# Twelve key pages instead of five handed out in layer 0's w_out, and the second sixteen hand-outs moved from page 200 to page 212

## The chip, the cores and the metric

The kernel runs on one core of one Trainium2 chip. The metric is the device time of one execution in microseconds: before the change 2924.34 us, the median of three runs (2919.79 to 2924.56). A core has a matrix engine (PE; PEld is its loading of weights), a vector engine (DVE), a scalar engine (ACT), GpSimd (POOL) and a sequencer that mostly issues DMA (SP). Each takes its instructions in the order in which they stand in its own list, and waits on semaphores for what the others have to finish first.

## The reference

One inference step of two layers over a prompt of 1024 tokens plus 16 meta tokens, and over 8 running sequences that add one token each. Layer 0 mixes with gated linear attention, layer 1 with differential attention; each is followed by a squared-ReLU MLP and post-norms. The part that the change touches is the attention of the 8 running sequences over their cached keys and values, 32 pages of 128 rows each, found through a page table. All is float32.

```python
def diff_core(q, k, v, q_pos, k_pos, lam):
    s = jnp.einsum('bqhmd,bkhmd->bhmqk', q, k).astype(F32) * (DIFF_DH ** -0.5)
    mask = k_pos[None, :] <= q_pos[:, None]
    s = jnp.where(mask, s, -jnp.inf)
    p = jax.nn.softmax(s, axis=-1)
    a = p[:, :, 0] - lam * p[:, :, 1]
    return jnp.einsum('bhqk,bkhe->bqhe', a, v.astype(F32))

def diff_sample(x, cache_k, cache_v, page_table, w_in, lam, lam_init, g_sub, w_out):
    ...
    k_past = cache_k[page_table].reshape(B, past, DIFF_HEADS, 2, DIFF_DH).astype(k.dtype)
    v_past = cache_v[page_table].reshape(B, past, DIFF_HEADS, DIFF_DV).astype(v.dtype)
    k_all = jnp.concatenate([k_past, k], axis=1)
    v_all = jnp.concatenate([v_past, v], axis=1)
    o = diff_core(q, k_all, v_all, pos, jnp.arange(past + T), lam)
```

## The kernel before

The prompt's work is matrix products of 128x128 tiles. Each float32 operand is split into a rounded high part and a rest (XH and XL, whi and wlo, HH and HL), and a product is three matmuls on these (`mm3`, L185 to L188). The stages in question follow each other: the output projection of layer 0 (`w_out`, 16 tiles), its post-norm and transposes (`normalize`, `to_fm`), layer 0's MLP (`mlp`, 8 groups, in each 8 tiles up and 16 down), the input projections of layer 1 (12 units of weights x 4 tiles, L1047 on), then differential attention over the prompt (`prep`, `tile_`). A tile is 48 matmuls of 256 columns, or 24 of 512, into one of three PSUM buffers (mmt). ACT and DVE take it out: L902 in w_out, the split into HH and HL (L183) for the MLP's first product, L1014 for its second, L1060 and the rope's L1068 to L1071 in the projections (for the units of queries and keys, the first 32 tiles).

Beside this runs the decode of the 8 sequences (`decode`). A key page is loaded (512 KB, `page`, L758, one of 8 buffers named pg), multiplied by the sequence's query row qb (L789; three of four pages on DVE, the fourth on POOL) and reduced to scores (L790, DVE). qb is one buffer: the row of the next sequence (L778) is loaded once the last multiply of the one before has read it. After 32 pages comes a softmax (`soft`: L795 a maximum on DVE, L797 and L801 on PE with L799 on DVE between, L802 on DVE, an exponential on ACT, L804 on DVE, L806 on PE, then L808 to L813 on DVE). The value pages of a sequence go with the key pages of the next: they are loaded into the same 8 buffers and multiplied by the weights on PE (L830). At the end of a sequence ACT, PE (L844) and DVE (L846) store its output. Keys are counted through: page 32 b + n is page n of sequence b, so 256 in all. SP reads each page's number from a table in memory (L756) before it issues its load; the tables and page buffers are given up when the projections end, and attention's tiles, among them its mask (cmask, L1102), take their place.

What sets the order: the program is written as one stream, and when it is built a scheduler lays it out on the engines by a simulated timeline. Decode's page work has the lowest priority, so it is put where an engine would otherwise have nothing. Where that comes too early, the source ties an instruction behind another one (`tc.issue_after`). `decode` is a generator, and handing out a page means that the prompt's code calls `next` on it once: in `w_out` after each of the first tiles, in the MLP's first group after every second tile of its second product (8 times), and in the projections after every tile. It stops (`yield`) before each page of sequence 0, and before 16 pages from HOLD on. A multiply of a page of sequence 0 up to page 23, and of a page of HOLD's sequence from HOLD's page on, is tied behind the latest step recorded in `steps_v` (L902, L1014, L1071 and others) at the time of its hand-out. After the MLP's first group the generator is run on to the first stop of HOLD, with no hand-outs between; after the 16th of the second set it runs to its end.

Of the kernel before, what the change touches and what calls it, by code (L numbers as in the profile page):

```python
# [30 lines left out]
NPG = 32  # L31
# [2 lines left out]
NEG = -1e30  # L34
LAM_INIT = 0.8 - 0.6 * math.exp(-0.3)
PGB = 8
HOLD = (6, 8)
HTB = 1
LEVELS = (64, 32, 16, 8, 4, 2, 1)
ROPE_INV = 500000.0 ** (-np.arange(0, 16, 2, dtype=np.float64) / 16)  # L40
# [70 lines left out]
def hybrid_step(ctx, tc, A, dbg=None, upto=9):  # L111
# [14 lines left out]
    def mmt():  # L126
        return mm.tile([P, 512], F32, name="mmt")
# [4 lines left out]
    def smt():  # L132
        return sm.tile([P, 512], F32, name="smt")
# [44 lines left out]
    def kunit(w, c0):  # L178
        return unit(256, w.rearrange("(k p) n -> p k n", p=P)[:, :, c0 : c0 + 256])
# [431 lines left out]
    for h in range(GH):  # L611
# [7 lines left out]
        for c in range(2):  # L619
# [3 lines left out]
            b = g2.tile([P, 512], F32, name="gb")  # L623
# [105 lines left out]
    @contextmanager  # L729
    def background():  # L730
        at = tc.cur_priority
        tc.cur_priority = bg_at[0]
        yield
        bg_at[0] = tc.cur_priority
        tc.cur_priority = at
# [17 lines left out]
    def page(cache, b, n):  # L753

        with tc.issue_after(gathers[-4]) if len(gathers) > 3 else nullcontext():
            r = nc.sync.value_load(ptab[b : b + 1, n : n + 1], min_val=0, max_val=A["cache_k"].shape[1] - 1)  # L756
        t = pgp.tile([P, D], F32, name="pg")
        gathers.append(dma(t, A[cache][0, ds(r, 1)].rearrange("a p h d -> (a p) (h d)")).ins)  # L758
        return t
# [14 lines left out]
    def k_start(b):  # L774
        sc = dp2.tile([P, NPG + 1, 16], F32, name="sc")
        qb = dp.tile([P, D], F32, name="qb")
        with background():
            dma(qb, A["qs"][b : b + 1, :].broadcast_to([P, D]))  # L778
            V.memset(sc[:, NPG, :], NEG)
            V.tensor_scalar(sc[:NS, NPG, :], own, other[:NS, b : b + 1], None, ALU.add)  # L780
        return sc, qb

    def k_page(b, n, sc, qb):
        with background():
            pg = page("cache_k", b, n)
            eng, after = (G, steps_g) if n % 4 == 3 else (V, steps_v)

            with tc.issue_after(after[-1]) if (b == 0 and n < 24 and after) or (b == HOLD[0] and HOLD[1] <= n) else nullcontext():
                eng.tensor_tensor(pg, pg, qb, op=ALU.mult)  # L789
            return V.tensor_reduce(sc[:, n, :], pg.rearrange("p (h d) -> p h d", d=64), op=ALU.add, axis=AX.X).ins  # L790

    def soft(sc):

        mx = dp.tile([P, 16], F32, name="mx")
        V.tensor_reduce(mx, sc.rearrange("p n c -> p c n"), op=ALU.max, axis=AX.X)  # L795
        ps = smt()
        TE.transpose(ps[:16, :P], mx, ident)  # L797
        m1 = dp.tile([16, 1], F32, name="m1")
        V.tensor_reduce(m1, ps[:16, :P], op=ALU.max, axis=AX.X)  # L799
        ps = smt()  # L800
        TE.matmul(ps[:, :16], m1.broadcast_to([16, P]), ident[:16, :16], start=True, stop=True)  # L801
        V.tensor_tensor(sc, sc, bc(ps[:, :16], [P, NPG + 1, 16], 1), op=ALU.subtract)  # L802
        S.activation(sc, sc, AF.Exp, scale=0.125)
        V.tensor_reduce(mx, sc.rearrange("p n c -> p c n"), op=ALU.add, axis=AX.X)  # L804
        ps = smt()
        TE.matmul(ps[:, :16], one, mx, start=True, stop=True)  # L806
        cf = dp.tile([P, 16], F32, name="cf")
        V.reciprocal(cf, ps[:, :16])  # L808
        cv = cf.rearrange("p (c m) -> p c m", m=2)
        V.tensor_tensor(cv, cv, bc(lamv, [P, 8, 2], 1), op=ALU.mult)  # L810
        V.tensor_tensor(sc, sc, bc(cf, [P, NPG + 1, 16], 1), op=ALU.mult)
        av = sc.rearrange("p n (c m) -> p n c m", m=2)
        V.tensor_tensor(av[:, :, :, 0], av[:, :, :, 0], av[:, :, :, 1], op=ALU.add)  # L813
        return sc
# [10 lines left out]
    def v_pages(pages, w, acc, behind):  # L825

        for n, pg in pages:
            r = slice(0, P if n < NPG else 32)
            for i in range(4):
                m = TE.matmul(acc[i * TS : i * TS + 16, :256], w[r, n, :], pg[r, i * 256 : (i + 1) * 256], start=n == 0, stop=n == NPG).ins  # L830
                if behind is not None:

                    tc.add_manual_dep(m, behind.name, mybir.DependencyInfo(mybir.DependencyClass.NoSync, mybir.DependencyReason.DATA), reason="order")
                    behind = None
# [13 lines left out]
    def decode():  # L848
        ks = None
        for b in range(NS + 1):  # L850
            prev = ks
            if b < NS:
                ks = k_start(b)
            if b > 0:
                w = soft(prev[0])
                acc = smt()
            held, k = [], None
            for n in range(NPG):
                if b == 0 or (b == HOLD[0] and HOLD[1] <= n < HOLD[1] + 16):
                    yield b  # L860
                if b < NS:
                    k = k_page(b, n, *ks)
                if b > 0:

                    if len(held) == 2:
                        v_pages(held, w, acc, k)
                        held = []
                    held.append((n, v_load(b - 1, n)))
            if b > 0:
                held.append((NPG, v_load(b - 1, NPG)))  # L870
                v_pages(held, w, acc, None)
                v_end(b - 1, acc)
# [9 lines left out]
    def w_out(w, scaled, side=None):  # L882

        units = {}
        n = 0
        for u, c in ((0, 0), (1, 0), (0, 1), (1, 1), (2, 0), (3, 0), (2, 1), (3, 1)):
            if u not in units:
                units[u] = kunit(w, u * 256)
            hv, lv = (x.rearrange("p (k n) -> p k n", n=256) for x in units[u])
            for i2 in range(2):  # L890
                ps = mmt()
                t0 = 4 * c + 2 * i2
                for i in range(2):
                    a = slice((t0 + i) * P, (t0 + i + 1) * P)
                    for k in range(NB):
                        mm3(ps[:, i * 256 : (i + 1) * 256], XH[:, k, a], XL[:, k, a], hv[:, k, :], lv[:, k, :], k == 0, k == NB - 1)
                yv = Yt[:, t0 : t0 + 2, u * 256 : (u + 1) * 256]
                pv = ps.rearrange("p (i n) -> p i n", n=256)
                if scaled:
                    V.tensor_tensor(yv, yv, pv, op=ALU.add)  # L900
                else:
                    steps_v.append(V.scalar_tensor_tensor(yv, yv, ALPHA, pv, ALU.mult, ALU.add).ins)  # L902
                if side and (n == 4 if scaled else n < 5):
                    next(side)
                n += 1
                if u % 2:
                    for t in (t0, t0 + 1):
                        yield t, u // 2
# [663 lines left out]
```

## Time and profile before

| what | value |
| --- | --- |
| three runs | 2924.56, 2924.34, 2919.79 us |
| span of the profiled execution | 2919.67 us |
| mean granted PE clock | 0.976 |
| read from and written to HBM | 575.55 MB and 44.06 MB |

The span runs from the first to the last instruction of the profiled execution. It lies 0.12 us below the lowest of the three runs; the median lies 4.7 us above it. On the time axis of the profile w_out runs from about 525 to 615 us, the MLP from there to about 1440, the projections of layer 1 from about 1453 to 1785, and attention over the prompt follows. In a row of a timeline stand start, length, engine, source line and operands, and in brackets how long the engine was idle just before and what ended that. A row of waits gives the total, the number and the longest. In a group's row stand the busy time and the mean length of one in ns, then the idle time ahead.

### The profile page before, as it was taken

How to read it: one execution, taken by the hardware profiler on the slowest of the kernel's cores; microseconds unless marked ns; L12 is line 12 of the kernel's file. 1: busy time of each engine (PE TensorE's matmuls, PEld its weight loads, DVE VectorE, ACT ScalarE, POOL GpSimd, SP SyncE). 2: the span in 40 equal slices, each digit the busy share in tenths (PEclk: the TensorE clock that was granted, in tenths of full speed). 3: DMA queues.
4: the chain of work that ended last, by engine and by line, in shares of the span. 5: the costliest groups of instructions: out<-in, count | busy, mean ns of one | idle time of the engine just before them, and what ended most of it. 6: DMA issues, size and time to landing. Idle time of an engine off the chain costs nothing. (4 is left out here: it accounts for less than half of the span.)

```text
span 2919.7 us, 52085 instructions
## 1 busy us (share of the span) xinstructions
PE 2779.7 (95%) x19653; PEld 2277.6 (78%) x19653; DVE 1891.2 (65%) x2982; ACT 1044.1 (36%) x2075; POOL 1133.7 (39%) x867
## 2 busy tenths in 40 slices
PE   8889999999999999999999998889998999999997
PEld 5666767987777777777898896778888889797885
DVE  2564644457877777777667942788638855838478
ACT  3233453251222122122321112667524535335352
POOL 2230222233333334334233331132335766677664
PEclk9899999999999999999999998999999999999998
DMA  7557651514798988988387999363436778595893
GB/s 257 178 185 251 233 177 37 198 56 141 242 350 297 335 309 298 346 317 321 137 275 252 348 343 314 75 139 86 119 112 205 195 207 232 152 281 129 257 246 87
DMA packets 285366, 636.46 MB, mean 218 GB/s; under 512 B 25510, under 2 KB 141292, under 8 KB 273852
## 3 DMA queue, kind: packets, MB, share of 16 engines
q1 hardware_dynamic: 252716, 520.66, 51.6%
q0 software_dynamic: 32400, 112.50, 15.9%
q8 instruction: 154, 2.52, 0.4%
q14 instruction: 96, 0.79, 0.1%
HBM read 575.55 MB, written 44.06 MB: 212 GB/s over the span
## 5 line engine op out<-in xcount | busy, mean ns | idle before, releaser
L174 POOL TENSOR_TENSOR wlo<-raw,whi 128x512 fp32r<-128x512 f32 x256 | 360.0, 1419 | 744.0 <-ACT whi L173 670.8
L186 PE MATMUL mmt<-whi,XH 128*128 128x256 f32 (+1 forms) x1760 | 527.4, 302 | 2.9 <-ACT Y L310 2.0
L187 PE MATMUL mmt<-wlo,XH 128*128 128x256 f32 (+1 forms) x1760 | 527.8, 301 | 0.7 <-POOL wlo L174 0.7
L186 PE MATMUL mmt<-XH,whi 128*128 128x512 f32 (+1 forms) x1216 | 438.1, 361 | 7.4 <-DVE HL L183 7.2
L188 PE MATMUL mmt<-whi,XL 128*128 128x256 f32 x1536 | 437.2, 286 | 0.1
L188 PE MATMUL mmt<-XH,wlo 128*128 128x512 f32 (+1 forms) x1216 | 434.4, 358 | 0.0
L790 DVE TENSOR_REDUCE sc<-pg 128x16 f32<-128x1024 f32 x256 | 309.7, 1214 | 93.4 <-POOL pg L789 90.1
L173 ACT CAST whi<-raw 128x512 fp32r<-128x512 f32 x256 | 152.9, 619 | 578.4 <-PE mmt L188 191.1
L186 PEld LDWEIGHTS mmt<-whi,XH 128*128 128x128 f32 x1760 | 333.4, 190 | 30.1 <-issue 15.6
L187 PEld LDWEIGHTS mmt<-wlo,XH 128*128 128x128 f32 x1760 | 334.8, 190 | 28.2 <-issue 16.8
L187 PE MATMUL mmt<-XL,whi 128*128 128x512 f32 x768 | 307.3, 400 | 0.0
L188 PEld LDWEIGHTS mmt<-whi,XL 128*128 128x128 f32 x1536 | 292.1, 191 | 9.9 <-issue 8.8
L789 DVE TENSOR_TENSOR pg<-pg,qb 128x1024 f32<-128x1024 f32 x192 | 256.8, 1343 | 62.1 <-DMA pg<-in_cache_k 38.1
L186 PEld LDWEIGHTS mmt<-XH,whi 128*128 128x128 f32 x1216 | 231.7, 191 | 55.1 <-issue 13.7
L789 POOL TENSOR_TENSOR pg<-pg,qb 128x1024 f32<-128x1024 f32 x64 | 158.6, 2478 | 293.5 <-DMA pg<-in_cache_k 236.7
L188 PEld LDWEIGHTS mmt<-XH,wlo 128*128 128x128 f32 x1216 | 231.8, 191 | 35.8 <-issue 3.8
L186 PE MATMUL mmt<-whi,HH 128*128 128x512 f32 x512 | 205.6, 402 | 1.7 <-DVE Y L1014 1.7
L187 PE MATMUL mmt<-wlo,HH 128*128 128x512 f32 x512 | 204.7, 400 | 0.0
L188 PE MATMUL mmt<-whi,HL 128*128 128x512 f32 x512 | 203.9, 398 | 0.0
L187 PEld LDWEIGHTS mmt<-XL,whi 128*128 128x128 f32 x768 | 145.4, 189 | 39.6 <-issue 8.8
L1416 POOL TENSOR_TENSOR wlo<-RW,whi 128x512 fp32r<-128x512 f32 x96 | 156.3, 1749 | 37.1 <-ACT whi L1415 37.0
L1416 POOL TENSOR_TENSOR wlo<-rw,whi 128x512 fp32r<-128x512 f32 x92 | 147.7, 1674 | 41.4 <-ACT whi L1415 41.2
(441 smaller groups left out, 5769.3 us busy)
## 6 DMA issues: line engine op xcount, KB each, us to landing
pg<-in_cache_k SPq DMA_DIRECT2D x256, 512.0 KB, 6.0
pg<-in_cache_v SPq DMA_DIRECT2D x256, 512.0 KB, 6.0
XH<-xc POOLq DMA_DIRECT2D x42, 1032.0 KB, 7.9
raw<-in_mlp_w SPq DMA_DIRECT2D x164, 256.0 KB, 3.5
swt<-in_mlp_w SPq DMA_DIRECT2D x32, 1024.0 KB, 5.6
rw<-in_mlp_w SPq DMA_DIRECT2D x116, 256.0 KB, 3.8
RW<-in_mlp_w POOLq DMA_DIRECT2D x96, 256.0 KB, 6.0
xc<-XH POOLq DMA_DIRECT2D x14, 1032.0 KB, 6.8
```

Source lines behind the costliest of these rows:

```text
L173: S.copy(hi[:, c], raw)
L174: G.tensor_tensor(lo[:, c], raw, hi[:, c].bitcast(F32), op=ALU.subtract)
L186: TE.matmul(ps, ah, bh, start=first, stop=False)
L187: TE.matmul(ps, ah, bl, start=False, stop=False)
L188: TE.matmul(ps, al, bh, start=False, stop=last)
L789: eng.tensor_tensor(pg, pg, qb, op=ALU.mult)
L790: return V.tensor_reduce(sc[:, n, :], pg.rearrange("p (h d) -> p h d", d=64), op=ALU.add, axis=AX.X).ins
L1416: G.tensor_tensor(lo[:, k, :], t, hi[:, k, :].bitcast(F32), op=ALU.subtract)
```

## The change

```diff
-HOLD = (6, 8)
+HOLD = range(212, 228)
...
-            with tc.issue_after(after[-1]) if (b == 0 and n < 24 and after) or (b == HOLD[0] and HOLD[1] <= n) else nullcontext():
+            with tc.issue_after(after[-1]) if (b == 0 and n < 24 and after) or HOLD.start <= NPG * b + n < NPG * (HOLD.start // NPG + 1) else nullcontext():
                 eng.tensor_tensor(pg, pg, qb, op=ALU.mult)
...
-                if b == 0 or (b == HOLD[0] and HOLD[1] <= n < HOLD[1] + 16):
+                if b == 0 or NPG * b + n in HOLD:
                     yield b
...
-                if side and (n == 4 if scaled else n < 5):
+                if side and (n == 4 if scaled else n < 12):
                     next(side)
```

In `w_out` of layer 0 `next` is called after 12 tiles, before after 5. The first call only starts the generator, so 11 key pages are handed out there (pages 0 to 10), before 4. The 8 calls in the MLP's first group then hand out pages 11 to 18, before 4 to 11. The second set of 16 is pages 212 to 227, before 200 to 215; it now goes over the change from sequence 6 to sequence 7 at page 224. Tied behind a step are pages 212 to 223, before 200 to 223.

No instruction is added or removed; the order on the engines changes. Counted in DVE's list by reduces (L790): ahead of the last tile of w_out stand 11 of them, before 4; ahead of the end of the MLP's first group 25, before 14; of its second group 46, before 39; of its end 212, before 200; of the projections' tile 12 there are 224, before 212; of tile 16 231, before 216; of tile 32 255, before 240.

The first place is DVE at the end of the MLP's first group. L1014 takes out its last tile and the HL rows are the splits of the second group's first tiles; pg and sc are decode's. Before:

```order
L1014 TENSOR_TENSOR Y<-Y,mmt 128x512 x2
L789 TENSOR_TENSOR pg<-pg,qb 128x1024 x8
L790 TENSOR_REDUCE sc<-pg 128x16 x5
L183 TENSOR_TENSOR HL<-mmt,HH 128x512
L790 TENSOR_REDUCE sc<-pg 128x16 x3
L183 TENSOR_TENSOR HL<-mmt,HH 128x512
```

and now:

```order
L1014 TENSOR_TENSOR Y<-Y,mmt 128x512
L789 TENSOR_TENSOR pg<-pg,qb 128x1024 x3
L790 TENSOR_REDUCE sc<-pg 128x16
L789 TENSOR_TENSOR pg<-pg,qb 128x1024
L790 TENSOR_REDUCE sc<-pg 128x16 x4
L183 TENSOR_TENSOR HL<-mmt,HH 128x512
L790 TENSOR_REDUCE sc<-pg 128x16 x2
L183 TENSOR_TENSOR HL<-mmt,HH 128x512
```

Between the last L1014 and the first HL there were eight multiplies and five reduces, and there are four and five; the multiplies taken out stand among the rows ahead.

The second place is DVE at the change from sequence 6 to 7, in the projections; qo, qr are the rope's tiles, m is the softmax's maximum. Before, at tile 21 to 24:

```order
L799 TENSOR_REDUCE m_17598<-smt 16x1
L789 TENSOR_TENSOR pg<-pg,qb 128x1024 x2
L1068 TENSOR_TENSOR qo<-mmt,c_rope 128x8x16
L1069 TENSOR_TENSOR qr<-mmt,c_rope 128x8x8
L1070 TENSOR_TENSOR qr<-mmt,c_rope 128x8x8
L802 TENSOR_TENSOR sc<-sc,smt 128x528
L790 TENSOR_REDUCE sc<-pg 128x16
L789 TENSOR_TENSOR pg<-pg,qb 128x1024
L790 TENSOR_REDUCE sc<-pg 128x16
L1071 TENSOR_TENSOR qo<-qo,qr 128x8x16
L804 TENSOR_REDUCE mx<-sc 128x16
```

and now, at tile 12 to 13:

```order
L795 TENSOR_REDUCE mx<-sc 128x16
L789 TENSOR_TENSOR pg<-pg,qb 128x1024
L1068 TENSOR_TENSOR qo<-mmt,c_rope 128x8x16
L1069 TENSOR_TENSOR qr<-mmt,c_rope 128x8x8
L1070 TENSOR_TENSOR qr<-mmt,c_rope 128x8x8
L1071 TENSOR_TENSOR qo<-qo,qr 128x8x16
L779 MEMSET sc 128x16
L790 TENSOR_REDUCE sc<-pg 128x16
L780 TENSOR_SCALAR sc<-own,c_other 8x16
L789 TENSOR_TENSOR pg<-pg,qb 128x1024
L790 TENSOR_REDUCE sc<-pg 128x16
L789 TENSOR_TENSOR pg<-pg,qb 128x1024
```

with L846 and L799 right behind. The first multiply by sequence 7's query row stood behind L799, and now stands behind L795 and ahead of L799 and of a rope. On PE 35 matmuls of the projections stand between L797 and L801 there, and 45 between L801 and L806.

The third place is the end of the projections on PE; axt rows are the transposes for attention's heads, L1174 and L1175 its first scores. Before:

```order
L188 MATMUL mmt<-whi,XL_86 128x256
L1134 MATMUL axt<-c_ident,whi 128x16
L1139 MATMUL axt<-c_ident,wlo 128x128 x4
L830 MATMUL smt<-pg,sc 16x256 x4
L1144 MATMUL axt<-c_ident,wlo 128x128 x4
L830 MATMUL smt<-pg,sc 16x256 x4
```

and now:

```order
L188 MATMUL mmt<-whi,XL_86 128x256
L1134 MATMUL axt<-c_ident,whi 128x16
L1139 MATMUL axt<-c_ident,wlo 128x128 x4
L1144 MATMUL axt<-c_ident,wlo 128x128 x4
L1139 MATMUL axt<-c_ident,wlo 128x128 x4
L1144 MATMUL axt<-c_ident,wlo 128x128 x4
L1174 MATMUL mmt<-XH_83 128x352
```

Sixteen value pages stood behind the last projection matmul, and none does now: the last page stands at tile 42, and L844 at tile 42.65. On DVE at the same place the splits of both heads stood ahead of L846, before:

```order
L813 TENSOR_TENSOR sc<-sc 128x264
L183 TENSOR_TENSOR XL_85<-axt,XH_83 128x16
L183 TENSOR_TENSOR XL_85<-axt,XH_83 128x512 x4
L1102 MEMSET cmask 128x320
L183 TENSOR_TENSOR XL_86<-axt,XH_84 128x16
L183 TENSOR_TENSOR XL_86<-axt,XH_84 128x512 x4
L846 COPY oT<-smt 128x4 x2
L1182 ISA as,ast<-mmt,cmask 128x352
```

and now:

```order
L813 TENSOR_TENSOR sc<-sc 128x264
L1102 MEMSET cmask 128x320
L846 COPY oT<-smt 128x4 x2
L183 TENSOR_TENSOR XL_85<-axt,XH_83 128x16
L183 TENSOR_TENSOR XL_85<-axt,XH_83 128x512 x4
L1182 ISA as,ast<-mmt,cmask 128x352
L1182 ISA ast 128x1
L183 TENSOR_TENSOR XL_86<-axt,XH_84 128x16
```

The mask and L846 have moved ahead of head 0's splits, and head 1's splits stand among attention's first score rows (L1182). Sequence 7's softmax (L797 on PE) stands at tile 33.4, before at tile 43.5.

## The prediction

> **What bounds the kernel now.** I read the page first, then busy time by stretch over the stages that the change touches, then what TensorE waited for in each, then the timelines at the three places where it waited.
>
> ```profile
> PE 2779.7 (95%) x19653; PEld 2277.6 (78%) x19653; DVE 1891.2 (65%) x2982; ACT 1044.1 (36%) x2075; POOL 1133.7 (39%) x867
> ...
> 500.00:640.00 140.00, 139.43 (x1018) 131.32 (x1017) 69.52 (x116) 52.81 (x83) 35.56 (x27) 1.00 0.38 128
> 640.00:706.00 66.00, 63.99 (x274) 51.21 (x273) 43.18 (x46) 14.33 (x26) 23.31 (x14) 1.00 0.38 120
> 706.00:780.00 74.00, 67.49 (x282) 53.10 (x280) 70.22 (x63) 21.32 (x37) 31.70 (x16) 0.98 0.64 222
> 780.00:1440.00 660.00, 659.68 (x3804) 481.20 (x3803) 486.57 (x535) 156.73 (x274) 242.92 (x150) 1.00 0.84 304
> 1440.00:1580.00 140.00, 139.65 (x1218) 129.21 (x1218) 91.75 (x145) 39.69 (x66) 45.20 (x30) 1.00 0.71 227
> 1580.00:1625.00 45.00, 39.69 (x297) 35.75 (x298) 38.47 (x56) 9.04 (x18) 14.29 (x10) 0.85 0.86 304
> 1625.00:1785.00 160.00, 160.00 (x1502) 140.85 (x1501) 83.13 (x95) 24.84 (x45) 46.47 (x27) 1.00 0.98 352
> 1785.00:1815.00 30.00, 18.24 (x176) 9.55 (x174) 6.76 (x16) 6.87 (x15) 5.31 (x11) 0.78 1.08 319
> ```
>
> After the stretch and its length stand the busy times of PE, its weight loads, DVE, ACT and POOL, then granted clock, DMA share and GB/s. PE is the bound: moving its work gains nothing, only its idle and slow time can be won. w_out (500 to 640), the bulk of the MLP (780 to 1440) and 1440 to 1580 hold 1.2 us of idle together, so nothing is to be had there. It sits at the start of the second MLP group (74 - 67.49 = 6.5), in the projections where the rest of the pages is let loose (45 - 39.69 = 5.3, clock 0.85) and between the last projection and attention (30 - 18.24 = 11.8, clock 0.78).
>
> **The change part by part.** *w_out.* Seven more pages are multiplied and reduced there.
>
> ```profile
> L790 DVE TENSOR_REDUCE sc<-pg 128x16 f32<-128x1024 f32 x256 | 309.7, 1214 | 93.4 <-POOL pg L789 90.1
> L789 DVE TENSOR_TENSOR pg<-pg,qb 128x1024 f32<-128x1024 f32 x192 | 256.8, 1343 | 62.1 <-DMA pg<-in_cache_k 38.1
> L789 POOL TENSOR_TENSOR pg<-pg,qb 128x1024 f32<-128x1024 f32 x64 | 158.6, 2478 | 293.5 <-DMA pg<-in_cache_k 236.7
> ...
> 544.27 7.24 SPq L758 DMA_DIRECT2D pg<-in_cache_k  x4
> ...
> 556.63 0.69 DVE L902 SCALAR_TENSOR_TENSOR Y<-Y,mmt 128x512 f32<-128x512 f32 x1 [4.89 <-PE mmt L188]
> 562.33 0.69 DVE L902 SCALAR_TENSOR_TENSOR Y<-Y,mmt 128x512 f32<-128x512 f32 x1 [3.68 <-PE mmt L188]
> ```
>
> Pages 4 to 10 are 7 reduces and 5 DVE multiplies, 7 x 1.21 + 5 x 1.34 = 15.2 us, and 2 on POOL. DVE's idle in this stretch, 140 - 69.5, holds it: one page costs 2.6 us per tile where DVE waited 3.7 to 4.9 us for PE. POOL, busy 35.6 of 140, takes its two at 2.48 us ahead of weight splits. The loads of pages 0 to 11 were issued by 551.5, so they wait for no DMA. On SP the loads of pages 12 on now stand among the weights. Taken at 0; if such a load held back a weight, the nearest price is the 2.0 us that PE lost in 640 to 706. Bounds 0 to +2: PE idles 0.6 us there, so no gain.
>
> *Second MLP group.* What makes PE wait is DVE, with pages queued ahead of the HL that frees a PSUM tile:
>
> ```profile
> 706.63 0.69 DVE L1014 TENSOR_TENSOR Y<-Y,mmt 128x512 f32<-128x512 f32 x1 [2.11 <-PE mmt L188]
> 707.23 13.57 DVE L789 TENSOR_TENSOR pg<-pg,qb 128x1024 f32<-128x1024 f32 x8
> 720.73 5.71 DVE L790 TENSOR_REDUCE sc<-pg 128x16 f32<-128x1024 f32 x5
> 726.36 0.67 DVE L183 TENSOR_TENSOR HL<-mmt,HH 128x512 fp32r<-128x512 f32 x1
> ...
> 727.09 0.79 PE L186 MATMUL mmt<-XH,whi 128*128 128x512 f32 x1 [3.77 <-DVE HL L183]
> ```
>
> Eight multiplies (1.70 each in this run) and five reduces (1.14) put the first HL at 726.4; PE had wanted the tile 3.77 us before 727.09, at 723.3. In the new order four multiplies and five reduces stand there: 4 x 1.70 + 5 x 1.14 = 12.5, so HL comes near 719.8 and PE does not wait. The next HL stand two reduces, two multiplies, then six instructions apart, under 8 us each, and three PSUM tiles of 5.7 us (556.63 to 562.33 above; the same 12288 columns) cover that. Of the 6.5 I leave 0.5 for a remnant and add 1 us for PE at half rate behind the wait (its first matmul above takes 0.79 us): -7. Bounds -7.5 and 0 (the backlog, 21 reduces in this group where there were 25, holds another HL).
>
> *Change of sequence.* Some 10 us are lost from 1580 to 1625: 5.3 are waits, the rest PE at half rate behind each.
>
> ```profile
> 1587.27 1.06 PE L830 MATMUL smt<-pg,sc 128*16 128x256 f32 x8 [2.56 <-DMA pg<-in_cache_v]
> ...
> 1588.63 0.42 PE L187 MATMUL mmt<-wlo,XH 128*128 128x256 f32 x1
> 1588.85 0.41 PE L188 MATMUL mmt<-whi,XL 128*128 128x256 f32 x1
> ...
> 1593.55 0.29 PE L186 MATMUL mmt<-whi,XH 128*128 128x256 f32 x1
> ...
> 1594.65 0.28 PE L186 MATMUL mmt<-whi,XH 128*128 128x256 f32 x1
> 1594.77 0.28 PE L187 MATMUL mmt<-wlo,XH 128*128 128x256 f32 x1
> ...
> 1598.08 0.37 SPq L778 DMA_DIRECT2D qb<-qs  x1
> ...
> 1604.86 2.36 DVE L789 TENSOR_TENSOR pg<-pg,qb 128x1024 f32<-128x1024 f32 x2 [5.64 <-DMA qb<-qs]
> ...
> 1614.85 0.61 PE L806 MATMUL smt<-mx,one 128*128 128x16 f32 x2 [2.75 <-DVE mx L804]
> ```
>
> A matmul takes 0.42 instead of 0.28 us, and starts come 0.22 instead of 0.12 apart, for 5.3 us after the first wait (1588.25 to 1593.55), a loss of 2.4; I take the same after the second: 5.3 + 4.8 = 10.1. Sequence 6's keys now end at tile 12, while hand-outs still pace the loads (227 GB/s and no such wait from 1440 to 1580), so the value pages that go with them should be there: the 2.56 and its slow time go, -5. The qb load stays: issue to landing is 6.8 us above, and the new order puts the multiply that needs it ahead of L799 and L802, where it stood between them. L799 is then some 4.3 us of waiting (6.8 less a reduce and L795) and 7 us of other DVE work behind L795, where PE has 35 projection matmuls (35 x 0.12 = 4.2 us) between L797 and L801. A wait of up to 7 us takes the place of the 2.75. Value taken: PE reaches L797 some 3 us late, so 4 us wait, near what is lost there now: 0. Part: -5, bounds -10 to +5.
>
> The Trainium skill, "TensorE: Matmul & The Clock Gate", section "What's actually happening", has the half clock as the state after an idle window of about 3.4 us. The trace differs: waits of 2.56 and 2.75 us brought it too. By the page the first wait costs 2.56 alone and this part would be -2.6 us instead of -5.
>
> *Last projection to attention.*
>
> ```profile
> 1741.45 1.08 DVE L795 TENSOR_REDUCE mx<-sc 128x16 f32<-128x528 f32 x1
> 1785.21 0.59 ACT L1060 COPY qo<-mmt 128x512 f32<-128x512 f32 x1 [8.12 <-PE mmt L188]
> 1789.98 0.42 PE L1174 MATMUL mmt<-XH 64*128 64x352 f32 x1
> 1802.22 0.33 DVE L1102 MEMSET cmask<- 128x320 f32 x1 [11.56 <-SPq L756]
> 1802.62 1.12 PE L1139 MATMUL axt<-c_ident,wlo 128*128 128x128 f32 x4 [7.35 <-DVE XL L183]
> 1814.31 0.53 DVE L1182 CUSTOM_DVE_ANT_0 as<-mmt,cmask 128x352 f32<-128x352 f32 x1 [0.32 <-DVE oT L846]
> ...
> L830 PE MATMUL smt<-pg,sc x128: 373/386/635, 1785.8 to 1810.9; 128*16 128x256 f32 x120, 32*16 32x256 f32 x8
> ...
> L830 PE MATMUL smt<-pg,sc 128*16 128x256 f32 (+1 forms) x616 | 42.0, 388 | 2.6 <-DMA pg<-in_cache_v 2.6
> ```
>
> Scores stand in PSUM from 1790.6, yet DVE takes the first at 1814.3: it waits at L1102 for SP's last page number (L756), then for the last sequence's output (L846). In the new order sequence 7's softmax is ten tiles earlier, its last value page at tile 42 of 48 and L846 ahead of head 0's splits. So 23.7 us go; but 16 value pages (128 of the rows, 8 a page) at 42.0/77 = 0.55 us now run among the projections, 8.8 us of PE, and head 1's five splits (3 us of DVE) share attention's start: 23.7 - 8.8 - 3 = 11.9. The idle of 11.8 says the same. Taken -12, bounds -15 (faster clock as well) and 0 (decode ends late still).
>
> *Do the pages arrive?*
>
> ```profile
> pg<-in_cache_v SPq DMA_DIRECT2D x69, 512.0 KB, 5.4
> raw<-in_diff_w_in SPq DMA_DIRECT2D x25, 256.0 KB, 6.1
> ...
> 1600.00:1785.00 185.00, 182.25 (x1663) 162.74 (x1662) 103.27 (x124) 29.16 (x52) 52.32 (x30) 0.98 0.97 346
> ```
>
> From tile 12 to the last value page: 97 pages (50.9 MB), weights of 8 units (8.4), outputs of 30 tiles (7.9, sized as a weight load) and some 5.5 of residual and small loads: 72.7 MB, less about 3 loaded ahead. PE's own work over it: 30 tiles x 48 matmuls x 0.12 = 173, 66 value pages x 0.55 = 36: 209 us. That asks 333 to 348 GB/s of queues that gave 346. Taken +2, bounds 0 to +9 (69.7 MB at 320).
>
> Sum: 0 - 7 - 5 - 12 + 2 = -22. The rest of the MLP is paced alike (186 reduces from the first group's end, now 187): 0. The profiled span 2919.7 is the lowest of the runs shown (2919.79); on it that is 2897.7, on the median 2924.34 it is **2902 us**.
>
> **The rivals.** *A: part of it is given back.* The qb wait at tile 12 costs its 7 us, or another HL waits: two of the terms gone, -22 + 5 + 7 = -10, 2914. For it: L789 stands ahead of L799; against: the changes of sequence within 780 to 1440 cost PE nothing.
> *B: nothing to measure.* Decode ends behind the last tile again and late pages cost 7 us ahead of it: -7 - 5 + 7 = -5, 2919. Against: decode ended 26 us behind that tile (1810.9 to 1785.2), and 15 key and 15 value pages of lead at tile 16 (216 reduces, now 231) are 15.7 MB, 45 us at 346 GB/s.
> *C: slower.* Value pages stand in PE's queue ahead of projections, where before 16 came behind the last one; a late page now stops the projections. Below 69.7/(209 + 24) = 299 GB/s the waits eat the other terms' 24 us. The 304 of 1580 to 1625 speaks for it; at 280 the wait is 40 us, 16 more than they win: 2940. Against: 346 and 352 over the 185 and 160 us of the same mix.
> *D: it does not do what it says:* the seven pages wait for loads in w_out and stall it. The loads' times above speak against; under 2 in 100, counted with C.
>
> **How the numbers follow.** The forecast, -15 to -33, 0.59; A 0.20; B 0.11; C (with D) 0.10. A measurement tells about 0.2%, 5.8 us, from no change: faster 0.79 (forecast and A), same 0.11, slower 0.10. Best ends: 7.5 + 10 + 15 = 33, 2891; with 3 us of spread between runs, 2888. Upwards the range takes in A and most of B: 2921.
>
> **What would show it.** Right: idle near 0 from 706 to 780, the last L846 before the last L1060, L1102 without a wait, scores to L1182 within a microsecond, PE idle by some 20 us less from 700 to 1815. Wrong: PE L830 waits on in_cache_v of over 10 us among the projections, L801 waiting for L799 at the change to sequence 7, or new waits for HL later in the MLP.

## The result, and the profile after

| | kernel before | changed kernel |
| --- | --- | --- |
| median of 9 runs | 2919.82 us (2915.06 to 2929.24) | 2902.84 us (2897.76 to 2912.84) |
| ratio | | 0.9939, 95% interval 0.9927 to 0.9951 |
| span of the profiled execution | 2919.7 us | 2896.0 us |

The ratio makes 17.8 us (14.3 to 21.3) of 2919.8. The time forecast, 2902, was met; the gain forecast was 22 us, on a median of three runs that lay 4.5 us above that of nine. So the terms have to be looked at one by one. The traces that follow differ by more than the ratio does, by 23.7 us: the profiled run of the changed kernel was the fastest of its nine (2897.76), that of the kernel before lies at the median of its nine (2919.79). Busy time by stretch of the changed kernel, in the columns of the prediction's rows:

```profile
500.00:640.00 140.00, 139.15 (x1014) 130.84 (x1014) 85.31 (x129) 51.90 (x82) 41.86 (x30) 1.00 0.48 160
640.00:706.00 66.00, 63.98 (x270) 51.18 (x269) 45.51 (x47) 14.97 (x27) 23.45 (x14) 0.97 0.39 122
706.00:780.00 74.00, 69.38 (x336) 53.56 (x335) 62.23 (x58) 21.48 (x37) 25.86 (x15) 0.95 0.64 220
780.00:1440.00 660.00, 660.00 (x3825) 479.07 (x3824) 502.09 (x535) 154.11 (x269) 245.05 (x151) 1.00 0.87 317
1440.00:1580.00 140.00, 138.56 (x1187) 126.71 (x1185) 101.00 (x166) 44.52 (x75) 47.81 (x33) 1.00 0.72 242
1580.00:1625.00 45.00, 45.00 (x419) 40.46 (x418) 40.47 (x53) 7.18 (x13) 17.20 (x10) 1.00 0.98 358
1625.00:1785.00 160.00, 160.00 (x1459) 137.88 (x1458) 51.75 (x71) 26.34 (x50) 36.05 (x27) 1.00 0.78 277
1785.00:1815.00 30.00, 26.67 (x134) 22.44 (x134) 18.60 (x56) 13.97 (x31) 4.69 (x9) 0.66 0.86 203
```

PE's idle time fell most from 1580 to 1625 (5.3 to 0) and from 1785 to 1815 (11.8 to 3.3), hardly from 706 to 780 (6.5 to 4.6), and there the clock is lower, 0.95 against 0.98 before. I call **loss** of a stretch its idle time plus its length times what the clock lacks to 1.00. From 640 to 780 it was 2.0 + 6.5 + 1.5 = 10.0 us and is 2.0 + 2.0 + 4.6 + 3.7 = 12.3; from 1440 to 1625 it was 12.4 and is 1.4. A clock printed to 0.01 leaves such a sum open by up to 0.9 us, and two profiles of one kernel (e10_spread2_hold8 and e12_repeat below) differ by 1.1 and 0.2 us in these two sums. The end of the projections is read from four lines of the kernel (count, shortest, middle and longest ns, first and last start) and one row of DVE's timeline:

```profile
L1060 ACT COPY qo<-mmt x48: 579/587/597, 1466.2 to 1787.5; 128x512 f32<-128x512 f32 x48
L846 DVE COPY oT<-smt x16: 152/155/166, 863.7 to 1757.2; 128x4 f32<-128x4 f32 x16
L1102 DVE MEMSET cmask<- x1: 325/325/325, 1728.5 to 1728.5; 128x320 f32 x1
L1182 DVE CUSTOM_DVE_ANT_0 as<-mmt,cmask x128: 288/508/647, 1794.0 to 2043.7; 128x272 f32<-128x272 f32 x32, 128x400 f32<-128x400 f32 x32, 128x352 f32<-128x352 f32 x16, 128x464 f32<-128x464 f32 x16
...
1728.55 0.33 DVE L1102 MEMSET cmask<- 128x320 f32 x1 [37.62 <-SPq L756]
```

Decode's last output (L846, 1757.2) is copied out 30 us ahead of the last projection's copy (L1060, 1787.5), and the first masked scores (L1182) follow 6.5 us behind that; before it was 1814.3 behind 1785.2, 29.1 us. The 16 value pages that stood there cost PE 8.8 us wherever they stand, so 29.1 - 8.8 - 6.5 = 13.8 us of loss are gone. The changes in loss add up to 2.3 - 11.0 - 13.8 = -22.5. In the traces the first masked scores come 20.3 us earlier (1814.3 to 1794.0), so the sums miss some 2 us; the other 3.4 of the 23.7 between the spans fall into attention, behind the first scores.

Why the second MLP group gained nothing is seen in DVE's timeline:

```profile
709.82 2.04 DVE L789 TENSOR_TENSOR pg<-pg,qb 128x1024 f32<-128x1024 f32 x1
711.79 0.68 DVE L1014 TENSOR_TENSOR Y<-Y,mmt 128x512 f32<-128x512 f32 x1
...
715.15 0.67 DVE L1014 TENSOR_TENSOR Y<-Y,mmt 128x512 f32<-128x512 f32 x1
715.75 6.89 DVE L789 TENSOR_TENSOR pg<-pg,qb 128x1024 f32<-128x1024 f32 x3
722.56 1.21 DVE L790 TENSOR_REDUCE sc<-pg 128x16 f32<-128x1024 f32 x1
723.69 1.21 DVE L789 TENSOR_TENSOR pg<-pg,qb 128x1024 f32<-128x1024 f32 x1
724.82 4.58 DVE L790 TENSOR_REDUCE sc<-pg 128x16 f32<-128x1024 f32 x4
729.33 0.67 DVE L183 TENSOR_TENSOR HL<-mmt,HH 128x512 fp32r<-128x512 f32 x1
```

Four multiplies and five reduces stand between the last L1014 and the first HL, as the order showed, and take 13.6 us. But that L1014 starts at 715.15, before at 706.63: DVE is behind when it comes there, and HL is later than before (729.3, 726.4).

### The profile page after: what moved, and what is told of

Same layout as the page of the kernel before. It is cut to its first block, busy times and chain, and to the rows that moved or that the text cites. A ratio compares the mean times of both kernels' runs of the same rounds, so it can differ in the third digit from the quotient of the medians.

```text
span 2896.0 us, 52075 instructions
## 1 busy us (share of the span) xinstructions
PE 2773.3 (96%) x19653; PEld 2267.4 (78%) x19653; DVE 1882.9 (65%) x2982; ACT 1043.5 (36%) x2075; POOL 1132.4 (39%) x867
## 5 line engine op out<-in xcount | busy, mean ns | idle before, releaser
L790 DVE TENSOR_REDUCE sc<-pg 128x16 f32<-128x1024 f32 x256 | 309.5, 1214 | 62.5 <-POOL pg L789 59.3
L188 PEld LDWEIGHTS mmt<-whi,XL 128*128 128x128 f32 x1536 | 289.8, 189 | 13.5 <-issue 11.8
L789 DVE TENSOR_TENSOR pg<-pg,qb 128x1024 f32<-128x1024 f32 x192 | 263.7, 1375 | 53.4 <-DMA pg<-in_cache_k 38.2
L186 PEld LDWEIGHTS mmt<-XH,whi 128*128 128x128 f32 x1216 | 230.6, 190 | 54.8 <-issue 14.6
```

What stands on the lines that cost most here:

```text
L186: TE.matmul(ps, ah, bh, start=first, stop=False)
L188: TE.matmul(ps, al, bh, start=False, stop=last)
```

## The experiments

Each kernel was timed against the kernel before on the same chip; edits are shown against the changed kernel. The sums beside the ratios, in us, are from each kernel's one profiled run (pages behind: value pages that PE multiplies behind the last projection; the column after it is the time from the last L1060 to the first L1182, less 0.55 for each of them; attention is the time from the first L1182 to the end of the span):

| kernel | ratio (95%) | loss 640 to 780 | loss 1440 to 1625 | pages behind | last projection to scores | attention |
| --- | --- | --- | --- | --- | --- | --- |
| before | 1 | 10.0 | 12.4 | 16 | 20.3 | 1105.4 |
| changed | 0.9939 (0.9927 to 0.9951) | 12.3 | 1.4 | 0 | 6.5 | 1102.0 |
| e1_wout_alone | 0.9997 (0.9982 to 1.0012) | 12.4 | 11.2 | 16 | 21.4 | 1107.7 |
| e2_hold_alone | 0.9961 (0.9946 to 0.9976) | 10.7 | 7.9 | 0 | 6.7 | 1106.5 |
| e3_hold8 | 0.9936 (0.9914 to 0.9958) | 12.6 | 0.4 | 0 | 6.7 | 1106.1 |
| e4_fc1 | 1.0009 (0.9995 to 1.0022) | 5.4 | 16.7 | 0 | 7.0 | 1114.3 |
| e5_spread | 0.9954 (0.9941 to 0.9966) | 14.6 | 8.9 | 0 | 6.5 | 1099.2 |
| e6_h208 | 0.9962 (0.9949 to 0.9975) | 10.3 | 8.1 | 2 | 9.1 | 1105.1 |
| e7_h219 | 0.9968 (0.9951 to 0.9985) | 12.2 | 6.7 | 0 | 6.9 | 1105.5 |
| e8_h206 | 0.9968 (0.9955 to 0.9981) | 10.9 | 10.5 | 8 | 9.5 | 1115.1 |
| e9_spread2 | 0.9937 (0.9922 to 0.9951) | 7.3 | 8.8 | 0 | 6.6 | 1108.1 |
| e10_spread2_hold8 | 0.9920 (0.9902 to 0.9937) | 5.6 | 6.8 | 0 | 6.5 | 1100.4 |
| e11_tie32 | 0.9945 (0.9931 to 0.9959) | 10.0 | 5.4 | 0 | 6.6 | 1103.3 |
| e12_repeat (e10's kernel again) | 0.9926 (0.9906 to 0.9946) | 6.7 | 7.0 | 0 | 6.8 | 1104.2 |

Attention's order changed as well, which the section on the change does not list: leaving value pages aside, some 560 of PE's 6769 instructions from the first L1174 on, and some 300 of DVE's 1397 from the first L1182 on, stand elsewhere than before. Kernels in which both lists are the same (before and e1_wout_alone; changed and e3_hold8; e2_hold_alone and e7_h219; e5_spread, e10_spread2_hold8 and e12_repeat) differ by 1 to 5 us there, so only the 1114 and 1115 of e4_fc1 and e8_h206 stand out, and each of these two has an order of its own. The profiled run of e8_h206 is the slowest of its five, 11.6 us above their median.

**Each half of the change alone.**

```diff
-HOLD = range(212, 228)
+HOLD = range(200, 216)      # e1_wout_alone
...
-                if side and (n == 4 if scaled else n < 12):
+                if side and (n == 4 if scaled else n < 5):      # e2_hold_alone
```

> Only w_out's part: twelve calls there, the second set of hand-outs at page 200 as before. The prediction on record: -7 us against the kernel before (HL near 719.8, no wait of PE behind 706), a ratio of 0.9976. The theory from the two traces: nothing, 0 to +2 us, 1.000 to 1.001: with seven pages more ahead only pages 19 to 23 are tied behind the group's last Y, three of the eight page buffers are free for untied pages, these run ahead of the last Y (715.1 instead of 706.6), and the first HL is as late as before (729 against 726); PE's wait of 4.6 us and the half clock behind it stay. Rival: the seven pages of lead carry on through the MLP and decode's end comes earlier too, -10 or more.

> Only the second set of hand-outs moved to page 212, five calls in w_out as before. The prediction on record: its terms for this part are -5 - 12 + 2 = -15 us, a ratio of 0.995. The theory from the two traces: the whole gain, -20 to -25 us, 0.9915 to 0.993, since first scores come 20.3 us earlier and attention gains 3.4 more. Rival: the twelve pages more that the MLP has to take need the seven from w_out; without them key or value pages are late, PE waits on in_cache_v or DVE on in_cache_k, and less than half of the gain is left, 0.997 or above.

w_out's half alone gains nothing: 0.9997, which is the theory from the two traces within the interval, and the 7 us on record fell. The second set alone is worth 11.4 us (7.0 to 15.8). That lies between the 15 on record and the rival's 9 or less, and the interval holds both; the whole gain that the theory gave it, 20 us or more, fell. The rival's mechanism is the one that the trace shows. The two halves make 12.3 us apart and 17.8 together; the intervals alone do not prove the difference, but the trace of e2_hold_alone shows where PE loses 6.5 us more than in the changed kernel. Busy time by stretch at the MLP's end:

```profile
1430.00:1450.00 20.00, 20.00 (x127) 14.42 (x126) 18.73 (x29) 5.05 (x6) 5.48 (x4) 1.00 0.93 306
1450.00:1460.00 10.00, 7.20 (x46) 5.95 (x46) 8.27 (x17) 7.57 (x13) 4.81 (x5) 0.98 0.64 232
1460.00:1470.00 10.00, 9.24 (x67) 9.06 (x66) 4.06 (x6) 6.26 (x9) 5.22 (x5) 0.85 0.34 101
```

and the same in the changed kernel:

```profile
1430.00:1450.00 20.00, 20.00 (x100) 16.41 (x99) 13.41 (x27) 8.27 (x11) 1.39 (x2) 1.00 0.09 33
1450.00:1460.00 10.00, 10.00 (x68) 9.04 (x67) 7.87 (x16) 5.81 (x11) 4.98 (x5) 1.00 0.17 55
1460.00:1470.00 10.00, 9.98 (x85) 9.76 (x83) 4.78 (x10) 7.55 (x12) 3.29 (x3) 1.00 0.65 184
```

In the changed kernel the pages let loose in the MLP are all in by 1430 (33 GB/s). Without the seven of w_out they still come at 306 GB/s up to 1450, and DVE has them between the steps of the norm and the last L1014:

```profile
1442.78 1.23 DVE L789 TENSOR_TENSOR pg<-pg,qb 128x1024 f32<-128x1024 f32 x1 [1.26 <-DMA pg<-in_cache_k]
1443.92 1.21 DVE L790 TENSOR_REDUCE sc<-pg 128x16 f32<-128x1024 f32 x1
1445.05 0.68 DVE L923 BATCH_NORM_STATS2 bst<-Y 128x6 f32<-128x512 f32 x1
1445.65 0.67 DVE L1014 TENSOR_TENSOR Y<-Y,mmt 128x512 f32<-128x512 f32 x1
1446.24 1.21 DVE L790 TENSOR_REDUCE sc<-pg 128x16 f32<-128x1024 f32 x1
...
1448.03 1.21 DVE L790 TENSOR_REDUCE sc<-pg 128x16 f32<-128x1024 f32 x1
```

DVE even waits for a key page there (1.26). The norm, the transposes and their splits come late, and PE waits for them as the projections begin (2.1 us for an XH, 1.4 for XL in three waits), then runs at 0.85 of its clock. So w_out's seven pages do pay, some 800 us further on: they keep the 12 more that the MLP has to take from running past its end.

**A shorter second set.**

```diff
-HOLD = range(212, 228)
+HOLD = range(212, 220)      # e3_hold8
```

> As the changed kernel, but the second set is 8 pages long, 212 to 219: the lead at decode's end stays (last L844 at tile 41.7 of 48, in the changed kernel 42.6), while the change from sequence 6 to 7 (tile 10.5) now comes after the loads have been let loose, as in the kernel before. Theory: the pacing over the change of sequence is worth some 8 us (idle 5.3 and clock 0.85 from 1580 to 1625 before, 0 and 1.00 after), so 5 to 9 us slower than the changed kernel, a ratio to the kernel before of 0.996 to 0.997, and PE L830 waits on in_cache_v at tile 8 to 11. Rival: only the lead at decode's end counts; within 2 us of the changed kernel, 0.993 to 0.9945.

The rival's: the same time as the changed kernel, and 0.4 us lost from 1440 to 1625. The change of sequence does not need hand-outs that still go on; my reason for the value pages being there was the wrong one.

**Other places for the second set.**

```diff
-HOLD = range(212, 228)
+HOLD = range(208, 224)      # e6_h208
...
+HOLD = range(219, 235)      # e7_h219
...
+HOLD = range(206, 222)      # e8_h206
```

> As the changed kernel with the second set at page 208: the change of sequence at tile 16.7, 2 value pages (in the kernel before 16, in the changed kernel none) behind the last projection. Theory: the gain goes with the value pages behind the last projection; 2 of 16 leave an eighth of the loss there and the tail of decode (last copies and L846) behind the projections: from the last L1060 to the first L1182 10 to 14 us (29.1 before, 6.5 in the changed kernel), 4 to 8 us slower than the changed kernel, 0.9955 to 0.9965. Rival: the fixed tail, not the pages, makes the stretch; then nearly all of the loss stays, 20 us or more in the stretch, 0.998 or above.

> As the changed kernel with the second set at page 219: seven pages more for the MLP, as many as e2_hold_alone lacked. Theory from e2_hold_alone and e4_fc1: the MLP's loose pages then do not end before its last group does, and PE loses 8 to 12 us between L1014 number 112 and the projections' tile 5, with waits for XH or XL splits and the clock below 1.00 from 1450 to 1470; 6 to 12 us slower than the changed kernel, 0.996 to 0.998. Rival: more lead only helps or saturates (nothing behind the last projection either way), within 2 us of the changed kernel, 0.993 to 0.9945.

> As the changed kernel with the second set at page 206: the change of sequence at tile 19.6, 8 value pages behind the last projection. Theory: half of the pages, about half of the stretch's loss, 16 to 20 us from the last L1060 to the first L1182, and the change of sequence costs what it cost before (some 8 us of waits and half clock): 11 to 15 us slower than the changed kernel, 0.9975 to 0.999. Rival: as for e6_h208, the fixed tail sets it; 25 us or more in the stretch, 0.9995 or above.

With 2 value pages behind the last projection the scores start 10.2 us after it (expected 10 to 14), with 8 it is 13.9 (expected 16 to 20), with 16 it is 29.1 in the kernel before. e6_h208 lands in its range with the ratio too; e8_h206 lies below its range in both, faster than expected. The fixed tail as the rival had it falls, but so does the theory's even price for each page: less PE's own work the loss over the 6.5 without pages is 2.6 us at 2, 3.0 at 8, 13.8 at 16. Most of the price comes between 8 and 16.

e6_h208 lost more at its change of sequence than behind the projections:

```profile
PE smt L801 <- DVE m L799: 5.1, 1, 5.1
```

```profile
1554.66 1.06 DVE L795 TENSOR_REDUCE mx<-sc 128x16 f32<-128x528 f32 x1
...
1559.68 1.23 DVE L789 TENSOR_TENSOR pg<-pg,qb 128x1024 f32<-128x1024 f32 x1 [3.96 <-DMA qb<-qs]
...
1571.86 0.27 DVE L799 TENSOR_REDUCE m<-smt 16x1 f32<-16x128 f32 x1
```

The first row is PE's waits from 1500 to 1620, the others DVE's timeline. This is the wait that the prediction took at 4 us: the multiply that needs the new qb stands ahead of L799, waits 3.96 us for the load, and L799 comes 17 us behind L795; the rest of the 17 is DVE's other work between them (L970, a rope, a reduce and more multiplies). In the changed kernel the same pair cost PE 1.0 us, in e5_spread 4.0, in e3_hold8 nothing. A second row buffer, which could take the wait for the load out, was not tried.

e7_h219 bears out the reading of e2_hold_alone: seven pages more for the MLP, and 8.5 us slower than the changed kernel by the ratios (6 to 12 expected) although decode ends earlier (last L846 at 1737.4, in the changed kernel 1757.2). Its pages still come at 308 GB/s from 1450 to 1460, and PE waits 1.9 us for XL; the lower clock that was expected there did not come (1.00). More lead does harm once the MLP's loose pages run past its end.

**The first HL of the second group.**

```diff
-            with tc.issue_after(after[-1]) if (b == 0 and n < 24 and after) or HOLD.start <= NPG * b + n < NPG * (HOLD.start // NPG + 1) else nullcontext():
+            with tc.issue_after(after[-1]) if (b == 0 and n < 32 and after) or HOLD.start <= NPG * b + n < NPG * (HOLD.start // NPG + 1) else nullcontext():      # e11_tie32 and e4_fc1
...
-                    split(HH[:, 2 * u + m, cs], HL[:, 2 * u + m, cs], ps)
+                    lo = split(HH[:, 2 * u + m, cs], HL[:, 2 * u + m, cs], ps); g == 1 and (steps_v.append(lo.ins), next(side))      # e4_fc1
...
-            us = [None, None]
+            us = [None, None]; g == 1 and next(x for x in side if x)      # e4_fc1: behind the group's first product
...
-            if g == 0:      # behind the group's second product
+            if g < 0:      # e4_fc1: no longer here
                 next(x for x in side if x)
```

> As the changed kernel, but pages 19 to 26 are handed out one per tile behind the HL of the MLP's second group, and all of sequence 0's pages from the calls on are tied, so no untied page runs ahead of the first group's last Y and no burst stands ahead of the first HL. Theory: last L1014 of the first group back near 707, no wait of PE for HL from 706 to 780, clock 1.00 there; 6 to 8 us faster than the changed kernel, a ratio to the kernel before of 0.991 to 0.992. Rival: the 13 pages fewer by the end of the second group (40 reduces, in the changed kernel 53) come back later as waits for value pages at 340 GB/s or more; equal to the changed kernel or slower, 0.994 or above.

> As the changed kernel, but all pages of the first sequence are tied (n < 32), so that pages 24 on can no longer run through free buffers ahead of the first group's last Y; seven multiplies and six reduces then stand between that Y and the first HL, in the changed kernel four and five. Theory: the last Y comes at 707 instead of 715, the first HL still at 724 to 729, so PE waits for it as long as before and nothing is won at the second group; 3 reduces fewer ahead of its end cost up to 3 us at the MLP's end: 0 to 3 us slower than the changed kernel, 0.994 to 0.995. Rival: untied pages ahead of Y are what costs; HL comes before 722 and 4 us or more are won, 0.9925 or below.

e11_tie32 came out as the theory had it (0.9945). DVE's timeline:

```profile
704.08 0.68 DVE L1014 TENSOR_TENSOR Y<-Y,mmt 128x512 f32<-128x512 f32 x1
704.67 11.66 DVE L789 TENSOR_TENSOR pg<-pg,qb 128x1024 f32<-128x1024 f32 x6
716.26 2.33 DVE L790 TENSOR_REDUCE sc<-pg 128x16 f32<-128x1024 f32 x2
718.52 1.21 DVE L789 TENSOR_TENSOR pg<-pg,qb 128x1024 f32<-128x1024 f32 x1
719.65 4.58 DVE L790 TENSOR_REDUCE sc<-pg 128x16 f32<-128x1024 f32 x4
724.15 0.67 DVE L183 TENSOR_TENSOR HL<-mmt,HH 128x512 fp32r<-128x512 f32 x1
```

With pages 24 on tied as well, L1014 is back where it was and the burst stands behind it again; HL is no earlier and PE waits 4.3 us. In the changed kernel only pages 19 to 23 are still tied there, so three of the eight buffers let untied pages through ahead of L1014. Whichever side of it they stand, the same loose pages are ahead of HL.

e4_fc1 takes them away from HL. Its rows for the second group and for the MLP's end:

```profile
706.00:780.00 74.00, 72.58 (x311) 57.97 (x310) 46.20 (x44) 20.67 (x36) 25.92 (x15) 1.00 0.44 142
1440.00:1580.00 140.00, 130.29 (x1106) 113.33 (x1108) 104.32 (x166) 39.11 (x66) 47.57 (x31) 0.95 0.85 292
```

The wait is gone and the clock is 1.00, 7 us less loss from 640 to 780, although the last L1014 ahead of it stands at 712.4 and not near the expected 707. Then 13 pages are missing at the end of the group, at the MLP's end 6 are, and 15 us more than in the changed kernel are lost from 1440 to 1625: 1.0009, on the rival's side and far beyond a tie. The losses do not make the whole of it: the span is 28.4 us longer than the changed kernel's, and 12.3 of them fall into attention, whose order differs here. Whether the missing pages or that order costs more is not shown.

**Both at once: spread hand-outs without losing pages.**

```diff
-                if side and (n == 4 if scaled else n < 12):
+                if side and (n == 4 if scaled else n < 16):      # and n < 32 in the tie, in all three
...
+                    lo = split(...); steps_v.append(lo.ins); (g == 0 and m or g == 1 and 2 * (2 * u + c) + m < 5) and next(side)      # e5_spread
...
-            us = [None, None]
+            us = [None, None]; g == 1 and next(x for x in side if x)      # e5_spread
...
-            if g == 0:
+            if g < 0:      # in all three
...
+                    lo, q = split(...), 2 * (2 * u + c) + m; g == 1 and steps_v.append(lo.ins); [next(side) for _ in range((g == 0 and m) or 2 * (g == 1 and q < 2) or (g == 1 and q == 2))]; (g, q) == (1, 3) and next(x for x in side if x)      # e9_spread2
...
+HOLD = range(212, 220)      # e10_spread2_hold8: e9_spread2 and this
```

> The first sequence's hand-outs spread without losing pages: 15 pages in w_out, 4 in the first half of the MLP's first group, 8 in its second half, 5 in the first half of the second group, all tied; then let loose; second set at 212 as in the changed kernel. 51 reduces stand ahead of the second group's end (changed kernel 53, e4_fc1 40), 213 ahead of the MLP's end (212 and 206). Theory: e4_fc1 showed the HL wait gone (7 us earlier at the second group's first L1014, 10 us at tile 112) and lost it at the MLP's end for want of 13 pages; with the pages there the 7 to 10 us stay: a ratio to the kernel before of 0.990 to 0.9915 (the changed kernel 0.9939). Rival: what DVE and the loads take in early shows as waits of PE in w_out or the first group (HL, wlo): equal to the changed kernel, 0.993 to 0.995.

> As e5_spread, but nothing of the layer's scaling of Y (tied behind the last recorded step) is put behind the first group's splits, which made PE wait 8.6 us for Y there, and the second group hands out two pages behind each of its first two HL, so 54 reduces stand ahead of the second group's end and 108 ahead of the fourth's (changed kernel 53 and 108, e5_spread 51 and 105). Theory: no wait for HL behind 706, no wait for Y, as much lead as the changed kernel, so PE loses nothing more at the MLP's end: 5 to 9 us faster than the changed kernel, a ratio to the kernel before of 0.9905 to 0.9925. Rival: the two waits at the second group's start only move to where DVE is full next (first group, or the MLP's end); equal to the changed kernel within 2 us, 0.993 to 0.9945, or slower.

> e9_spread2 with the second set 8 pages long (212 to 219). Theory from e3_hold8, where the shorter set changed nothing: as e9_spread2 within 2 us, PE without a wait above 1 us at the change of sequence. Rival: the wait of L801 for L799 at the change of sequence (1.0 us in the changed kernel, 4 to 5 in e5_spread and e6_h208, none in e3_hold8) goes with where the change falls, and the shorter set saves 3 to 5 us.

> The kernel of e10_spread2_hold8 a second time, to tell whether it is faster than the changed kernel (0.9939, 0.9927 to 0.9951). If it is: 0.990 to 0.9925 again. If the 0.992 was spread between runs: 0.993 to 0.9945.

The rivals held in e5_spread and e9_spread2 (0.9954, a little slower than the rival's range, and 0.9937): no wait for HL is left, but PE waits for Y (L1014, 8.6 and 5.3 us from 640 to 780), and again from 1440 on. e10_spread2_hold8 has the lowest loss at the second group of the three:

```profile
640.00:706.00 66.00, 62.76 (x267) 50.30 (x266) 46.68 (x48) 16.95 (x30) 25.12 (x14) 0.97 0.41 130
706.00:780.00 74.00, 73.60 (x375) 56.43 (x374) 50.09 (x54) 21.10 (x37) 21.43 (x14) 1.00 0.57 200
1440.00:1580.00 140.00, 134.65 (x1148) 121.98 (x1147) 99.88 (x162) 41.86 (x71) 49.18 (x32) 0.99 0.74 258
```

It gave 0.9920 and in e12_repeat 0.9926 (0.9906 to 0.9946), medians 2901.09 and 2900.19 us; the second lies between the two ranges that were to tell them apart. Its wait of L801 for L799 is 1.3 us, 3.2 in e9_spread2, which speaks for the rival on the shorter set; the theory's bound of 1 us for that wait did not hold. Both ratios are below that of the changed kernel, but the intervals overlap: that it is faster is not shown. It wins some 6.7 us ahead of 780 and gives 5.3 of them back from 1440 on. Where its MLP loses at the end although it has as many pages done as the changed kernel (159 reduces are left behind the second group in both) stays open.

## Why the prediction came out, point by point

*w_out, 0.* Right: PE's idle time from 500 to 640 went from 0.6 to 0.9 us. The working has one slip: of pages 4 to 10 only page 7 is POOL's, so DVE got six multiplies more and not five (15.8 us more busy time, against 15.2).

*Second MLP group, -7.* This step failed: "In the new order four multiplies and five reduces stand there ... HL comes near 719.8 and PE does not wait." The rows were right, but their start was taken from the trace of before, 706.6. The multiplies that left the place stood in the rows ahead of it and made DVE 8.5 us late. The four and five rows themselves took 13.6 us and not 12.5. From 706 to 780 the loss was 8.0 us before and is 8.3; the other 2.0 by which the loss from 640 to 780 grew are a lower clock behind an earlier wait (last section). The half of the change that this term belongs to gained 0.9 us (-3.5 to 5.3, e1_wout_alone). The bound of 0 was the case, but not for the reason beside it: what held the first HL were the rows known from the order, and no other HL.

*Rest of the MLP, 0.* Right, and more was in it than the prediction saw. It counted 186 reduces from the first group's end before and 187 now. e2_hold_alone has 198 and e7_h219 194: both lose 5 to 7 us more than the changed kernel from 1440 to 1625. The seven pages of w_out are what keeps this term at 0. (To the second group's end the traces have 54 reduces, before 47, and not the 46 and 39 of the section on the change; the difference of 7 is the same.)

*Change of sequence, -5.* The sign was right and the size was not: 12.4 us of loss became 1.4. The wait for a value page went, as taken. The wait of L801 for L799 cost 1.0 us and not the 4 that stood for it; e6_h208 with 5.1 shows that the 4 were no phantom but depend on where the change falls. The reason given, that hand-outs pace the loads there, is refuted by e3_hold8. So where this gain is won is shown, and why is not: what makes the value pages late at tile 22 in the kernel before and not at tile 10 to 13 is left open.

*Last projection to attention, -12.* Right: -13.8 by the same sum, with the scores 6.5 us behind the last projection, and 6.5 to 7.0 in the eight experiments and the repeat in which no value page is left behind it. Two of the signs came otherwise than foretold. L1102 is not without a wait: DVE still waits there for SP's last page number, 37.6 us where it was 11.6, but this ends at 1728.5, 65 us ahead of the first scores, and so costs nothing. And from the end of the first L1175 to L1182 it is 2.5 us (1791.5 to 1794.0) and not one; before it was the 23.7 of the prediction.

*Do the value pages arrive, +2.* They do, so the term is 0, the lower end of its bounds: PE has no wait for in_cache_v in the projections, at 358 GB/s from 1580 to 1625. Rival C fell with it. The idle time from 706 to 1815 fell by 14.9 us (24.3 to 9.4) where some 20 were foretold.

So the likeliest case held in time and by the place that carried it. Its 22 us had one term of 7 that brought nothing, and one that brought 6 us more than was taken; that the two nearly cancel is luck. It is luck too that 2902 met the time: a gain 4 us too large was taken off a median 4.5 us too high. The ratio that it stood for, 2902 to 2924.34 or 0.9924, lies just outside the measured interval. Not in the sum at all was attention, whose order changed too: the stretch from the first L1182 to the end was 1102 us, before 1105, a difference that kernels with one and the same order there show as well.

## What to carry to other kernels

Rows that an order moves away from a place do not leave the engine: before a wait is called gone, add up all that the engine has to do from the last moment it was idle up to the row in question. An engine's free time early on can pay far behind, at the next place where a backlog has to be done by a deadline; count the work left to each deadline, and not only the rows at the wait. The count alone does not decide, as e10_spread2_hold8 shows, which loses at the MLP's end with no more work left than the changed kernel. And two halves of a change that look independent are worth running apart, since here one gained nothing alone and some 6 us beside the other.

## What the runs showed of the hardware

The same wait, PE's for an HL in the MLP's first group, was and was not followed by a lower clock. The stretch that holds it, in the kernel before and, in the next two fences, in the changed kernel and in e8_h206:

```profile
650.00:660.00 10.00, 7.99 (x34) 6.13 (x34) 5.14 (x6) 4.18 (x8) 5.26 (x4) 1.00 0.40 127
```

```profile
650.00:660.00 10.00, 7.98 (x28) 6.08 (x27) 5.35 (x7) 5.20 (x10) 5.58 (x4) 0.83 0.41 128
```

```profile
660.00:670.00 10.00, 7.62 (x34) 6.16 (x34) 5.90 (x7) 4.67 (x9) 4.48 (x3) 1.00 0.34 98
```

PE idled 2.01, 2.02 and 2.38 us; only the 2.02 was followed by the lower clock, with 28 matmuls in the stretch and not 34, some 1.4 us. A shorter wait was followed by it as well, L801's 1.58 us in e2_hold_alone:

```profile
1550.80:1554.80 4.00, 4.00 (x22) 3.97 (x23) 3.97 (x7) 0.88 (x2) 3.44 (x2) 0.62 1.05 409
```

So the length of a wait does not settle it in this range. The Trainium skill, "TensorE: Matmul & The Clock Gate", section "What's actually happening", says that the window which is watched runs freely and does not start anew with the kernel, so that it matters where in it a matmul falls; that fits these four, while its idle window of about 3.4 us does not fit waits of 1.58 and 2.02. For a sum this means that a wait of about 2 us costs itself, and perhaps a microsecond or two more.

A multiply of a page on DVE took 1.21 us in the changed kernel while POOL was idle (723.69), and 6.89 us for three at 715.75, where POOL worked from 714.7 to 721.6. A single one was dear too, 3.14 us at 702.76, beside a multiply of POOL's from 702.42 to 704.82, so it is POOL's work alongside and not the burst that goes with the longer time here. The prediction's 1.70 was the mean of eight, 13.57 us, of which POOL worked 9.0; for three that ran beside POOL nearly throughout it was too little.
